# Rows of an RMSNorm + SiLU kernel dealt out to partitions in another order: 64 consecutive rows for each partition

## The chip, the cores and the metric

The kernel runs on one core of one Trainium2 chip. The metric is the device time of one execution in microseconds (us); lower is better. Three runs of the kernel before took 316.70, 317.02 and 317.08 us, so its median is 317.02 us.

The engines that matter here are ScalarE (ACT in the profile), VectorE (DVE), SyncE (SP, which only issues transfers in this kernel) and the core's 16 DMA engines, which move all data between the device memory and the core's on-chip memory. The on-chip memory has 128 partitions. TensorE (PE) is used once, at the start, to copy one row to all partitions.

## The reference

```python
batch, seq_len, hidden = 8, 1024, 2048          # x: (8, 1024, 2048) float32, gamma: (2048,)

def reference(x, gamma, eps):
    rms = np.sqrt(np.mean(x ** 2, axis=-1, keepdims=True) + eps)
    out = gamma * x / rms
    return (out * (1 / (1 + np.exp(-out)))).astype(np.float32)
```

Flattened, x is an array of 8192 rows of 2048 float32 values, 8 KB a row and 67.1 MB in all. Each row is computed by itself: its root mean square, the division by it, the multiplication by gamma, and SiLU. The output has the same shape. So 67.1 MB are read and 67.1 MB are written, and any assignment of rows to partitions computes the same thing as long as the output is written by the same assignment.

## The kernel before, in words

**Tiling.** The 8192 rows are cut into `nblk` = 16 blocks. A block has 128 partitions with `J` = 4 rows each: 512 rows, 4 MB, in one tile `xt` of 128 x 8192 float32. Six such buffers exist (`BUFS` = 6). A load (`load`, line 54) brings one whole block in with one transfer, issued from ScalarE's queue; a store (`store`, line 102) writes one whole block out, issued from SyncE's queue. Results are written in place, so a store reads the buffer that the load filled.

**Where a block lies in memory.** Lines 35 and 36 give the views `xb` and `ob` of x and out. In the kernel before, the rows are numbered block first, then partition, then row in the partition. Partition p of block b holds the rows 512 b + 4 p to 512 b + 4 p + 3. Its four rows are one run of 32 KB, and the 128 runs of a block follow one another, so a block is one piece of 4 MB.

**Work on a block.** Each of a block's four rows per partition is squared and summed, some of them on ScalarE (`squares_scalar`, line 65) and some on VectorE (`squares_vector`, line 73). `root` (line 82) takes the square root of the mean on ScalarE, `invert` (line 87) the reciprocal on VectorE, `multiply` (line 92) multiplies each row by its reciprocal and by gamma on VectorE, and `silu` (line 98) applies SiLU on ScalarE in two halves of a block and then issues the store. The last block takes another form of the same arithmetic (lines 152 to 158), so that its store can be issued early.

**Order.** The order is written out by hand (`manual_schedule`). Load 0 is issued first, then gamma is loaded from SyncE's queue (line 110) and copied to all partitions by TensorE (line 113); load 1 and then loads 2 to 5 follow on ScalarE's queue. In the loop over blocks, the squares of block b + 1 stand beside the multiplication and SiLU of block b. Load b + 3 is issued by ScalarE behind its first squares of block b + 1 (line 69), from b = 3 on, into the buffer that the store of block b - 3 must have left.

Of the kernel before, what the change touches and what calls it, by code (L numbers as in the profile page):

```python
# [1 line left out]

# [4 lines left out]

ACT = mybir.ActivationFunctionType
ALU = mybir.AluOpType


@with_exitstack
def kernel(
    ctx: ExitStack,
    tc: tile.TileContext,
    x: bass.AP,
    gamma: bass.AP,
    eps: bass.AP,
    out: bass.AP,
):  # L20

    nc = tc.nc
    P = nc.NUM_PARTITIONS
    f32 = mybir.dt.float32
    x2 = x.flatten_outer_dims()
    o2 = out.flatten_outer_dims()  # L30
    n, d = x2.shape
    J = 4
    BUFS = 6
    nblk = n // (P * J)
    xb = x2.rearrange("(b p j) d -> b p (j d)", p=P, j=J)
    ob = o2.rearrange("(b p j) d -> b p (j d)", p=P, j=J)

    singles = ctx.enter_context(tc.tile_pool(name="singles", bufs=1))
    pool = ctx.enter_context(tc.tile_pool(name="pool", bufs=BUFS))
    small = ctx.enter_context(tc.tile_pool(name="small", bufs=2))  # L40
    psum = ctx.enter_context(tc.tile_pool(name="psum", bufs=1, space=bass.MemoryType.PSUM))

    Q = 4
    w = d // Q
    g = singles.tile([P, d], f32)
    eps_t = singles.tile([P, 1], f32)
    ones = singles.tile([P, P], f32)
    junk_a = psum.tile([P, d], f32, name="junk_a")
    junk_v = psum.tile([P, d], f32, name="junk_v")
    blocks, sss, rmss, rstds = {}, {}, {}, {}  # L50

    def load(b):
        xt = pool.tile([P, J * d], f32, name="xt")
        nc.scalar.dma_start(out=xt, in_=xb[b])  # L54
        blocks[b] = xt

    def row(b, j):
        return blocks[b][:, j * d:(j + 1) * d]

    def squares_scalar(b, loads=()):  # L60


        sss[b] = small.tile([P, J], f32, name="ss")
        for j in range(share(b)):
            nc.scalar.activation(out=junk_a, in_=row(b, j), func=ACT.Square,  # L65
                                 accum_out=sss[b][:, j:j + 1])
            if j == 0:
                for s in loads:
                    load(s)

    def squares_vector(b):
        for j in range(share(b), J):
            nc.vector.tensor_tensor_reduce(  # L73
                out=junk_v, in0=row(b, j), in1=row(b, j), scale=1.0, scalar=0.0,
                op0=ALU.mult, op1=ALU.add, accum_out=sss[b][:, j:j + 1])

    def share(b):
        return 1 if 4 <= b <= 12 and b % 2 == 0 else 2

    def root(b):  # L80
        rms = small.tile([P, J], f32, name="rms")
        nc.scalar.activation(out=rms, in_=sss.pop(b), func=ACT.Sqrt, scale=1.0 / d, bias=eps_t)  # L82
        rmss[b] = rms

    def invert(b):
        rstd = small.tile([P, J], f32, name="rstd")
        nc.vector.reciprocal(out=rstd, in_=rmss.pop(b))  # L87
        rstds[b] = rstd

    def multiply(b):  # L90
        for j in range(J):
            nc.vector.scalar_tensor_tensor(out=row(b, j), in0=row(b, j), scalar=rstds[b][:, j:j + 1],  # L92
                                           in1=g, op0=ALU.mult, op1=ALU.mult)

    def silu(b):
        for h in range(0, J, 2):
            cols = slice(h * d, (h + 2) * d)
            nc.scalar.activation(out=blocks[b][:, cols], in_=blocks[b][:, cols], func=ACT.Silu)  # L98
        store(b)

    def store(b):
        nc.sync.dma_start(out=ob[b], in_=blocks[b])

    with tc.manual_schedule():

        load(0)
        nc.vector.memset(ones, 1.0)  # L107
        nc.vector.memset(eps_t, float(eps))
        nc.scalar.activation(out=junk_a[:, 0:1], in_=ones[:, 0:1], func=ACT.Square)  # L109
        nc.sync.dma_start(out=g[0:1, :], in_=bass.AP(tensor=gamma.tensor, offset=gamma.offset, ap=[[d, 1], [1, d]]))  # L110
        for c in range(Q):
            cols = slice(c * w, (c + 1) * w)
            nc.tensor.matmul(junk_v[:, cols], ones[0:1, :], g[0:1, cols], start=True, stop=True)  # L113
        load(1)
        nc.vector.tensor_copy(out=g, in_=junk_v)  # L115
        nc.scalar.copy(out=junk_a[:, 0:1], in_=junk_v[:, d - 1:d])  # L116
        for b in range(2, BUFS):
            load(b)

        last = nblk - 1
        SOON = 3
        squares_scalar(0)
        squares_vector(0)
        root(0)
        invert(0)
        for b in range(last):
            loads = [b + 3] if BUFS <= b + 3 < nblk else []
            if b < SOON:  # L130
                multiply(b)
                squares_scalar(b + 1, loads)
                silu(b)
                squares_vector(b + 1)
                root(b + 1)
            elif b < last - 1:
                squares_scalar(b + 1, loads)
                squares_vector(b + 1)
                root(b + 1)
                multiply(b)  # L140
                silu(b)
            else:
                multiply(b)
                squares_scalar(b + 1)
                silu(b)
                squares_vector(b + 1)
                root(b + 1)
            if b + 1 < last:
                invert(b + 1)


        for j in range(J):
            if j == J // 2:
                invert(last)
            nc.vector.tensor_mul(out=row(last, j), in0=row(last, j), in1=g)  # L155
        for j in range(J):
            nc.scalar.activation(out=row(last, j), in_=row(last, j), func=ACT.Silu,  # L157
                                 scale=rstds[last][:, j:j + 1])
        store(last)


# [1 line left out]
_INS = ['x', 'gamma', 'eps']  # L163
_OUTS = [((8, 1024, 2048), 'float32')]

_NUMBERS = {'eps': 9.999999747378752e-06}


# [26 lines left out]
```

## Time and profile before

| | |
|---|---|
| time, median of 3 runs | 317.02 us (316.70 to 317.08) |
| profiled execution: its span, first to last instruction | 315.1 us |
| VectorE busy | 235.3 us (75%) |
| ScalarE busy | 213.9 us (68%) |
| bytes moved | 134.24 MB, mean 426 GB/s over the span |
| one load, issue to landing, median | 38.7 us |
| one store, issue to landing, median | 29.0 us |

The profile's page shows one execution. Its span is counted from the first to the last instruction, so the time that a run reports is a little longer: here 317.02 us at the median against a span of 315.1 us. The page gives no separate total time for the profiled execution.

How to read the lines that follow. The page's "busy" line has, for each engine, busy us, share of the span and number of instructions. The rows under the heading of 40 slices cut the span into 40 equal pieces of 7.88 us; a digit is the busy share in tenths, and the GB/s row has the bytes that landed in each slice. A line of the queues has the number of packets, the megabytes, and the time that the packets took as a share of 16 engines over the span; q10 carries the loads of x, q1 the stores and gamma. The chain is the series of waits and instructions that ended last, followed back from the end, as shares of the span. A line of the waits reads: engine, what was about to run and its line, what it waited for, us in total, how often, the longest.

### The profile page before, as it was taken

The page shows a single profiled execution, that of the slowest core. Times are in us where ns is not written, and L with a number is a line of the kernel's source. Part 1 is how long each engine was busy: PE and PEld are TensorE (multiplying, and loading weights), DVE is VectorE, ACT ScalarE, POOL GpSimd, SP SyncE. Part 2 cuts the span into 40 slices and gives each one's busy share as a digit, 9 for nine tenths or more (in the row PEclk, how much of TensorE's full clock was granted, in tenths as well). Part 3 has the DMA queues.
Part 4 walks back from the last instruction along what each step waited for, and adds up shares of the span by engine and source line. Part 5 has one row for each costly group of instructions (what it writes and reads, how often), then busy time and mean ns, then how long its engine had stood idle before and what let it go on. Part 6 is the DMA issues. An engine that isn't in the chain of part 4 may idle for free.

```text
span 315.1 us, 439 instructions
## 1 busy us (share of the span) xinstructions
PE 7.2 (2%) x8; PEld 2.5 (1%) x8; DVE 235.3 (75%) x157; ACT 213.9 (68%) x137; POOL 0.2 (0%) x4
## 2 busy tenths in 40 slices
PE   6200000000000000000000000000000000000000
PEld 2000000000000000000000000000000000000000
DVE  0679697979895695957969489593995939999600
ACT  1269998972799258682687827877278768779910
POOL 0000000000000000000000000000000000000000
DMA  8999999999999999999999999999999999999997
GB/s 334 412 453 416 383 458 408 462 403 462 403 459 408 454 412 458 408 462 403 462 403 462 408 458 408 458 408 458 416 449 416 449 416 449 428 437 428 437 428 308
DMA packets 4613, 134.24 MB, mean 426 GB/s; under 512 B 514, under 2 KB 514, under 8 KB 514
## 3 DMA queue, kind: packets, MB, share of 16 engines
q10 hardware_dynamic: 2304, 67.11, 49.8%
q1 hardware_dynamic: 2306, 67.12, 49.3%
q14 instruction: 3, 0.02, 0.0%
HBM read 67.12 MB, written 67.11 MB: 426 GB/s over the span
## 4 chain that ended last, share of the span: by engine, by line
DMA 68%; DVE 14%; ACT 11%; issue 1%; ACTq 1%; DVEq 0%
DMA xt<-in_x_dram 68%; DVE xt L92 9%; DVE junk_v L73 5%; ACT xt L98 4%; ACT junk_a L65 3%; ACT xt L157 2%; ACT L82 1%; ACTq L190 1%; ACT L157 0%; ACT L98 0%; ACT rms L82 0%; DVE ss L73 0%; ACTq L54 0%; DVE rstd L87 0%; ACT L109 0%
## 5 line engine op out<-in xcount | busy, mean ns | idle before, releaser
L92 DVE SCALAR_TENSOR_TENSOR xt<-xt,rstd,g 128x2048 f32<-128x2048 f32 x60 | 137.0, 2346 | 0.1
L98 ACT ACTIVATE xt<-xt 128x4096 f32<-128x4096 f32 x30 | 108.3, 3615 | 27.4 <-DVE xt L92 27.4
L73 DVE CUSTOM_DVE_ANT_0 junk_v<-xt 128x2048 f32<-128x2048 f32 x37 | 85.1, 2299 | 42.9 <-DMA xt<-in_x_dram 42.2
L65 ACT ACTIVATE junk_a<-xt 128x2048 f32<-128x2048 f32 x27 | 50.7, 1876 | 16.1 <-DMA xt<-in_x_dram 14.0
L82 ACT ACT_TABLE_LOAD x15 | 19.2, 1283 | 26.6 <-DVE ss L73 26.5
L98 ACT ACT_TABLE_LOAD x14 | 18.0, 1283 | 0.2
L115 DVE COPY g<-junk_v 128x2048 f32<-128x2048 f32 x1 | 2.3, 2292 | 9.0 <-PE junk_v L113 9.0
L87 DVE RECIPROCAL rstd<-rms 128x4 f32<-128x4 f32 x16 | 2.7, 172 | 8.4 <-ACT rms L82 8.4
L155 DVE TENSOR_TENSOR xt<-xt,g 128x2048 f32<-128x2048 f32 x4 | 8.9, 2277 | 0.0
L82 ACT ACTIVATE rms<-ss,eps_t 128x4 f32<-128x4 f32 x16 | 4.8, 297 | 5.7 <-DVE ss L73 5.5
L157 ACT ACTIVATE xt<-xt,rstd 128x2048 f32<-128x2048 f32 x4 | 7.7, 1991 | 0.0
L113 PE MATMUL junk_v<-g,ones 1*128 1x512 f32 x8 | 7.2, 1072 | 2.8 <-DMA g<-in_gamma_dram 2.8
L116 ACT COPY junk_a<-junk_v 128x1 f32<-128x1 f32 x1 | 0.1, 144 | 9.8 <-DVE g L115 9.8
L73 DVE DVE_READ_ACCUMULATOR2_ANT ss<- 128x1 f32 x37 | 5.2, 141 | 0.0
L65 ACT ACTIVATION_READ_ACCUMULATOR junk_a<-xt 128x1 f32 x27 | 5.0, 186 | 0.0
L113 PEld LDWEIGHTS junk_v<-g,ones 1*128 1x128 f32 x8 | 2.5, 325 | 5.9 <-issue 5.9
L109 ACT ACT_TABLE_LOAD x1 | 1.3, 1283 | 1.1 <-PEq L176 1.1
L157 ACT ACT_TABLE_LOAD x1 | 1.3, 1283 | 0.0
L107 DVE MEMSET ones<- 128x128 f32 x1 | 0.2, 165 | 0.8 <-PEq L176 0.8
L109 ACT ACTIVATE junk_a<-ones 128x1 f32<-128x1 f32 x1 | 0.2, 174 | 0.0
L176 POOL MEMSET const-bfloat16-1.0<- 128x1 bf16 x1 | 0.1, 103 | 0.0
L176 POOL MEMSET const-uint8-127<- 128x1 uint8 x1 | 0.1, 102 | 0.0
(3 smaller groups left out, 0.3 us busy)
## 6 DMA issues: line engine op xcount, KB each, us to landing
xt<-in_x_dram ACTq DMA_DIRECT2D x16, 4096.0 KB, 38.7
out_dram<-xt SPq DMA_DIRECT2D x16, 4096.0 KB, 29.0
g<-in_gamma_dram SPq DMA_DIRECT2D x1, 8.0 KB
```

Source lines behind the costliest of these rows:

```text
L65: nc.scalar.activation(out=junk_a, in_=row(b, j), func=ACT.Square, accum_out=sss[b][:, j:j + 1])
L73: nc.vector.tensor_tensor_reduce(out=junk_v, in0=row(b, j), in1=row(b, j), scale=1.0, scalar=0.0, op0=ALU.mult, op1=ALU.add, accum_out=sss ...
L82: nc.scalar.activation(out=rms, in_=sss.pop(b), func=ACT.Sqrt, scale=1.0 / d, bias=eps_t)
L87: nc.vector.reciprocal(out=rstd, in_=rmss.pop(b))
L92: nc.vector.scalar_tensor_tensor(out=row(b, j), in0=row(b, j), scalar=rstds[b][:, j:j + 1], in1=g, op0=ALU.mult, op1=ALU.mult)
L98: nc.scalar.activation(out=blocks[b][:, cols], in_=blocks[b][:, cols], func=ACT.Silu)
L109: nc.scalar.activation(out=junk_a[:, 0:1], in_=ones[:, 0:1], func=ACT.Square)
L113: nc.tensor.matmul(junk_v[:, cols], ones[0:1, :], g[0:1, cols], start=True, stop=True)
L115: nc.vector.tensor_copy(out=g, in_=junk_v)
L155: nc.vector.tensor_mul(out=row(last, j), in0=row(last, j), in1=g)
L157: nc.scalar.activation(out=row(last, j), in_=row(last, j), func=ACT.Silu, scale=rstds[last][:, j:j + 1])
L190: with _tile.TileContext(nc) as tc:
```

## The change

The two views are rearranged with the partition first, then the block, then the row in the partition.

```diff
     nblk = n // (P * J)
-    xb = x2.rearrange("(b p j) d -> b p (j d)", p=P, j=J)
-    ob = o2.rearrange("(b p j) d -> b p (j d)", p=P, j=J)
+    xb = x2.rearrange("(p b j) d -> b p (j d)", p=P, j=J)
+    ob = o2.rearrange("(p b j) d -> b p (j d)", p=P, j=J)
```

Now partition p holds the rows 64 p to 64 p + 63 over the whole kernel, and block b takes the rows 64 p + 4 b to 64 p + 4 b + 3 of every partition. A partition's share of a block is still one run of 32 KB. The starts of neighbouring partitions' runs are 64 rows apart, 512 KB, and no longer 32 KB. The runs of one block are spread over the whole array, and the next block's runs lie directly behind them. Loads and stores use the same assignment. Nothing else in the kernel is touched: the transfers are as many, of the same sizes, on the same queues and in the same order.

## The prediction

> **What bounds the kernel now.** I read the page of the profiled execution first (shares, transfers, chain), then the waits, then a table of the span cut into stretches.
>
> The page's opening, the transfer rows under the 40 slices, its queues and its chain:
>
> ```profile
> span 315.1 us, 439 instructions
> PE 7.2 (2%) x8; PEld 2.5 (1%) x8; DVE 235.3 (75%) x157; ACT 213.9 (68%) x137; POOL 0.2 (0%) x4
> ...
> DMA  8999999999999999999999999999999999999997
> GB/s 334 412 453 416 383 458 408 462 403 462 403 459 408 454 412 458 408 462 403 462 403 462 408 458 408 458 408 458 416 449 416 449 416 449 428 437 428 437 428 308
> DMA packets 4613, 134.24 MB, mean 426 GB/s; under 512 B 514, under 2 KB 514, under 8 KB 514
> ...
> q10 hardware_dynamic: 2304, 67.11, 49.8%
> q1 hardware_dynamic: 2306, 67.12, 49.3%
> ...
> DMA 68%; DVE 14%; ACT 11%; issue 1%; ACTq 1%; DVEq 0%
> ```
>
> The 16 DMA engines are busy in every slice but the first and the last, while VectorE (DVE) is busy for 75% and ScalarE (ACT) for 68% of the span. The chain that ended last is 68% loads. So the transfers set the pace. The waits say the same from the other side: the longest waits of the two computing engines on anything outside themselves are for loads.
>
> ```profile
> DVE junk_v L73 <- DMA xt<-in_x_dram: 42.2, 11, 5.7
> ...
> ACT junk_a L65 <- DMA xt<-in_x_dram: 14.0, 7, 2.7
> ```
>
> VectorE waits 42.2 us in 11 places for a block to land before its square sums on line 73, ScalarE 14.0 us in 7 places on line 65. Those waits are slack: if transfers slow down, the two engines wait longer and take nothing from anybody.
>
> Next, what one packet costs. The load queue q10 carries 2304 packets: 16 transfers of 128 data runs of 32 KB, and 16 small packets more for each transfer. Its share is 49.8% of 16 engines over 315.1 us, so 0.498 x 16 x 315.1 / 2048 = 1.226 us for a run that is loaded; for the store queue q1, 0.493 x 16 x 315.1 / 2048 = 1.214 us. Each engine handles 4096 / 16 = 256 runs, one after the other, and 256 x 1.21 = 310 us is nearly the span. Whatever changes the time of one 32 KB run changes the kernel's time 256 times over.
>
> The span cut into stretches (columns: from and to; width; busy us of PE, PEld, DVE, ACT, POOL; clock; DMA share; GB/s):
>
> ```profile
> 4.00:36.00 32.00, 5.94 (x7) 1.75 (x6) 20.95 (x14) 18.97 (x15) 0.00 (x0) 1.00 0.99 429
> 36.00:42.00 6.00, 0.00 (x0) 0.00 (x0) 5.17 (x4) 5.93 (x7) 0.00 (x0) 1.00 0.95 350
> 42.00:280.00 238.00, 0.00 (x0) 0.00 (x0) 192.53 (x128) 166.74 (x102) 0.00 (x0) 1.00 1.01 434
> 280.00:300.90 20.90, 0.00 (x0) 0.00 (x0) 16.46 (x11) 20.79 (x13) 0.00 (x0) 1.00 0.99 428
> ```
>
> From 4 to 36 us there are loads only (the first store is issued at 35.2 us): 429 GB/s. From 42 to 280 us loads and stores share the engines half and half: 434 GB/s. A read-only and a mixed stretch run at one rate, so in this layout the memory's mix of work does not set the 1.21 us; something the engines have in common does. The exception is the 6 us in which the first store joins: 350 GB/s at a DMA share of 0.95. That is 350 x 6 = 2.10 MB in place of 434 x 6 = 2.60 MB, a loss of 0.50 MB, or 1.16 us at 434 GB/s. The engines were hardly idle there, so the runs themselves took longer: 0.95 x 16 x 6 us over 2.10 MB / 32 KB = 64 runs gives 1.42 us for one. It is the one place where the trace shows a run slowed by something outside its engine.
>
> **The change, part by part.** Nothing is added or removed in the instruction streams: 16 load issues on ScalarE's queue and 16 stores on SyncE's, 128 runs of 32 KB each, in the same order and behind the same waits; VectorE, ScalarE and TensorE do the same work on the same tile shapes. These cost 0, without any cover being needed. The permutation of rows over partitions is the same for load and store. The row gamma is loaded as before. A partition's run stays whole at 4 rows = 32 KB, so I expect 2304 packets again.
>
> What changes is where the runs lie in memory. Before, the 128 runs of a transfer follow each other and fill one stretch of 4 MB. After, each starts 512 KB after the last, so a transfer touches the whole 64 MB array, and the 16 engines, which step through their runs together, always work at places that are equal modulo 512 KB up to their progress within a run. The proof that they step together is in the slices: the rate alternates between about 403 and 462 GB/s, which over 7.88 us is 3.18 and 3.64 MB, near 6 and 7 rounds of 16 runs of 32 KB (0.524 MB each). If the memory spreads its work by the address bits that the runs now have in common, the 16 engines crowd onto few of its parts.
>
> No row of this trace has runs at that pitch, so the price is bounded from both sides.
> - **Lower end.** The steady rate cannot rise by the change if the read-only stretch and the mixed one already agree to 1% with sequential runs. What can go is the dip at 36 to 42 us: -1.16 us. So the gain is at most about 1.2 us.
> - **Upper end.** Every run is as slow as those of the dip. 134.24 MB take 134.24 / 0.434 = 309.3 us at the steady rate and 134.24 / 0.350 = 383.5 us at the dip's: +74.2 us.
> - **The value taken.** The steady row holds 238 us, the dip 6 us, so the value must lie near the lower end. I put one run in eight at the dip's price, as if of the eight runs that an engine has in each transfer the first, at which it moves to a new part of the array, were the one that collides: 74.2 / 8 = 9.3 us. This eighth is a choice, not a reading; the ends are kept for the range.
>
> The Trainium skill speaks against the change. "DMA: Bandwidth & Descriptors", section "Latency and other measured facts", lists copies with 128 partitions of 16 KiB at a row pitch that is a large power of two: 207 GB/s in each direction at 512 KiB, 164 at 2 MiB, 103 at 4 MiB, against 214 with a padded pitch. No row of this trace has such a pitch. Taken as 207 against 214, the 309.3 us would become an estimated 319.8 us, +10.5 us, and the kernel 327.5 us. The page calls its explanation, engines in lock step that meet on the same channels of the memory, an inference.
>
> **The sum.** The profiled execution's span is 315.1 us; the median of the runs is 317.02 us, so 1.9 us lie around the span. 315.1 + 9.3 = 324.4 us of span, and 324.4 + 1.9 = 326.3 us. Call it 326 us. What the span holds beside the 309.3 us (its start, the dip, the last receipt: 5.8 us) is taken as unchanged.
>
> **The rivals.**
> - **The memory has room: no change.** For it: 429 and 434 GB/s in stretches with unlike work, and runs that hold 1.21 us for 240 us together. Against it: those rows have sequential runs only, and the dip shows that the memory side can stretch a run. It gives 317.0 us, within 0.2% (0.6 us, about what a measurement of this kernel can tell from no change).
> - **The dip goes: faster.** Place: 36 to 42 us, where the first store joins the loads. Price: 1.16 us. Before, load and store streams lie in separate 4 MB pieces; spread over the arrays they may meet more evenly. It gives 317.02 - 1.16 = 315.9 us. It decides only as long as the steady rate holds: at 434 x 309.3 / (309.3 + 1.16) = 432.4 GB/s the gain is used up. Against it: the dip may be the store queue's start and no matter of addresses.
> - **The crowding is general: much slower.** If half of the runs pay the dip's price, 74.2 / 2 = 37.1 us, 354 us; all of them, 391 us. For it: the pitch is the same in every transfer, load and store, so nothing within a transfer cures it. Against it: a 32 KB run passes over many small addresses within 1.21 us, and engines that are held up fall out of step and then collide less.
> - **The change does not do what it says.** If the runs were cut differently, for instance at a row of 8 KB, the packets would be four times as many; there are already 514 small packets in 315 us without a visible price. The contiguous inner 32 KB speaks against it.
>
> **How the numbers follow.** Chances: the forecast, with its own range from one run in sixty to one run in four at the dip's price (+1.2 to +18.6 us, 318 to 336 us), 0.50; no change 0.16; the dip goes 0.12; general crowding, above 336 us, 0.20; other cuts, slower, 0.02. So faster 0.12, same 0.16, slower 0.72. The range of 315.5 to 354 us, from the faster rival to half of the runs at the dip's price, holds nearly all of the first three cases and half of the fourth, some 0.87 in all; to cut it shorter would leave out either the faster rival or the crowding, whose price nothing in the trace pins down.
>
> **What would show it right or wrong.** Right: 2304 packets on q10 again, the DMA row of the slices still full, but the stretch from 42 to 280 us near 421 GB/s (434 x 309.3 / 318.6) and each queue's time per run near 1.25 us; the waits of line 73 for loads longer, VectorE's and ScalarE's busy time as before. The no-change rival shows 434 GB/s and 1.21 us; the faster one shows 434 with the 36 to 42 us stretch filled; general crowding shows a rate under 400 GB/s. The prediction is wrong if the rate holds in every stretch, or if a queue's shares diverge, loads slowed and stores not, so that the price falls on one direction alone: then half of the sum, some 4.6 us, would be left.

## The result and the profile after

The changed kernel takes 322.03 us (median of 6 runs, 319.94 to 323.86) against 317.03 us for the kernel before (6 runs, 316.70 to 317.15). The ratio is 1.016, with a 95% interval of 1.0146 to 1.0174: 5.0 us slower. The runs also lie further apart than before, 3.9 us from lowest to highest against 0.45 us.

The profiled execution of the changed kernel is the slowest of the six: 323.86 us, with a span of 322.1 us. So its trace shows 7.0 us more span than that of before, 2.0 us more than the median lost; what is split up below are these 7.0 us. The page's opening, the rows under the 40 slices, the queues and the chain:

```profile
span 322.1 us, 439 instructions
PE 7.2 (2%) x8; PEld 2.5 (1%) x8; DVE 235.4 (73%) x157; ACT 214.1 (66%) x137; POOL 0.2 (0%) x4
...
DMA  8999999999999999999999999999999999996994
GB/s 318 427 427 435 387 419 435 440 415 440 431 420 444 423 420 444 423 435 431 431 431 427 431 435 419 435 431 435 431 423 423 431 444 411 427 435 301 444 403 203
...
q10 hardware_dynamic: 2304, 67.11, 49.3%
q1 hardware_dynamic: 2306, 67.12, 48.3%
...
DMA xt<-in_x_dram 69%; DVE xt L92 8%; ACT xt L98 5%; DVE junk_v L73 5%; ACT junk_a L65 3%; ACT xt L157 2%; ACT L82 1%; ACTq L190 1%; ACT L157 0%; ACT L98 0%; ACT rms L82 0%; DVE ss L73 0%; DVE rstd L87 0%; ACTq L54 0%; ACT L109 0%
```

Three things are to be seen. The packets are the same in number, 2304 and 2306, so the transfers were cut as before. The engines' busy time is the same (VectorE 235.4, ScalarE 214.1 us). And the GB/s row has lost its pattern: before, it alternated between about 403 and 462, a sign of 16 engines that finish their 32 KB runs together; now it wanders around 430, a sign of engines out of step. (Late in the kernel before the pattern fades too, to 428 and 437, so it is no proof; the landings below are better evidence.) Near the end stands a hole (a DMA digit of 6, 301 GB/s) that the kernel before does not have.

The shares turn into time per run as in the prediction: a loaded run takes 0.493 x 16 x 322.1 / 2048 = 1.241 us (1.226 before), a stored run 0.483 x 16 x 322.1 / 2048 = 1.215 us (1.214 before). Only loads got slower, by 0.015 us on average. Over the 128 loaded runs of an engine that is 1.9 us, not 7.

The same stretches as before (columns: from and to; width; busy us of PE, PEld, DVE, ACT, POOL; clock; DMA share; GB/s), changed kernel:

```profile
4.00:36.00 32.00, 6.08 (x8) 1.90 (x6) 20.96 (x14) 18.56 (x15) 0.00 (x0) 1.00 1.00 433
36.00:42.00 6.00, 0.00 (x0) 0.00 (x0) 4.76 (x4) 5.94 (x7) 0.00 (x0) 1.00 0.98 350
42.00:280.00 238.00, 0.00 (x0) 0.00 (x0) 187.16 (x127) 163.37 (x102) 0.00 (x0) 1.00 1.00 430
280.00:300.90 20.90, 0.00 (x0) 0.00 (x0) 19.84 (x12) 17.85 (x11) 0.00 (x0) 1.00 0.91 390
```

As long as only loads run, the new layout costs nothing: 433 GB/s from 4 to 36 us, where the kernel before had 429. The dip at 36 to 42 us is there again, at 350. The steady stretch has 430 in place of 434, the stretch from 280 us on 390 in place of 428.

Where the 7.0 us come from shows in the chain of waits in order of time. Each piece is the time (start, us) in which the chain ran through loads alone; the three last pieces of before, then of after:

```profile
143.81 38.65 DMA xt<-in_x_dram
182.50 38.67 DMA xt<-in_x_dram
...
240.56 38.64 DMA xt<-in_x_dram
```

```profile
146.45 39.16 DMA xt<-in_x_dram
205.48 40.28 DMA xt<-in_x_dram
245.79 40.35 DMA xt<-in_x_dram
```

In such a piece two blocks are loaded and two stored; it has grown from 38.65 to as much as 40.35 us. The last starts 5.2 us later than before and ends at 286.14 us (245.79 + 40.35) against 279.20 us (240.56 + 38.64): 6.9 us later. What follows, the arithmetic of the last block and its store, takes 322.1 - 286.1 = 36.0 us and took 315.1 - 279.2 = 35.9 us. So the whole loss is the later landing of the last load.

Each load ends in the trace with 16 small packets of 4 bytes, which are read here as one for each engine, sent when its part is done. For the last load of the kernel before, all 16 stand in a window from 276.5 to 278.9 us:

```profile
DMA packets 48, 1.05 MB, mean 437 GB/s; under 512 B 16, under 2 KB 16, under 8 KB 16
...
q10 hardware_dynamic: 16, 0.00, 0.4%
```

They start from 278.01 to 278.85 us there, and from 277.08 to 285.77 us after the change. The first is even earlier than before; the last is 6.9 us later, and it is the last that the waiting engines go by (the chain has the landing at 286.14 us). Before, the spread between the first and the last is never over 0.8 us. After, it is 0.8 us at the first load, 4.4 at the eighth, 5.5 at the twelfth, 8.7 us at the last: some parts fall further and further behind. The queues of the changed kernel in the 6.7 us after 279.2 us, when before all loads were done and no packet of q10 was left:

```profile
DMA packets 105, 2.95 MB, mean 440 GB/s; under 512 B 15, under 2 KB 15, under 8 KB 15
...
q10 hardware_dynamic: 13, 0.20, 6.8%
```

0.20 MB are 6 runs that late engines still have to load, and everything waits for them. At the other end, engines that were not late run out of work. Changed kernel, two short stretches near the end:

```profile
294.00:298.00 4.00, 0.00 (x0) 0.00 (x0) 3.83 (x2) 3.98 (x2) 0.00 (x0) 1.00 0.38 164
...
318.70:320.80 2.10, 0.00 (x0) 0.00 (x0) 0.00 (x0) 0.00 (x0) 0.00 (x0) 1.00 0.04 16
```

From 294 to 298 us the engines are 38% busy, since the earlier stores are out and the last blocks' arithmetic is late. From 318.7 us on a share of 0.04 is less than one engine of 16: the rest wait for the last one. Put together by the shares, the 16 engines were busy with the two queues for 97.6% of 322.1 = 314.4 us after and 99.1% of 315.1 = 312.3 us before. Of the 7.0 us, 2.1 are longer runs and 4.9 are engines that have nothing to do.

### The profile page after: what moved, and what is told of

The parts are those of the page before. It is cut to its first block, busy times and chain, and to the rows that moved or that the text cites. A ratio compares the mean times of both kernels' runs of the same rounds, so it can differ in the third digit from the quotient of the medians.

```text
span 322.1 us, 439 instructions
## 1 busy us (share of the span) xinstructions
PE 7.2 (2%) x8; PEld 2.5 (1%) x8; DVE 235.4 (73%) x157; ACT 214.1 (66%) x137; POOL 0.2 (0%) x4
## 3 DMA queue, kind: packets, MB, share of 16 engines
q10 hardware_dynamic: 2304, 67.11, 49.3%
q1 hardware_dynamic: 2306, 67.12, 48.3%
## 4 chain that ended last, share of the span: by engine, by line
DMA 69%; DVE 14%; ACT 12%; ACTq 1%; issue 1%; DVEq 0%
DMA xt<-in_x_dram 69%; DVE xt L92 8%; ACT xt L98 5%; DVE junk_v L73 5%; ACT junk_a L65 3%; ACT xt L157 2%; ACT L82 1%; ACTq L190 1%; ACT L157 0%; ACT L98 0%; ACT rms L82 0%; DVE ss L73 0%; DVE rstd L87 0%; ACTq L54 0%; ACT L109 0%
```

## The experiments

**One side at a time.** Which transfers must have the new layout for the price to appear? First the stores alone, then the loads alone.

```diff
-    ob = o2.rearrange("(b p j) d -> b p (j d)", p=P, j=J)
+    ob = o2.rearrange("(p b j) d -> b p (j d)", p=P, j=J)
```

> Loads as before (one piece of 4 MB), stores as in the change (runs 512 KB apart); each result row is thus written at the place of another row. In the changed kernel only the load runs took longer (1.24 us against 1.226 by the queue's share), and only from the moment the first store had joined. Theory C (it is the scattered stores that hold up loads): 322 us, last load landing near 286 us, loads' time per run near 1.24 us. Theory D (it is the loads' own pitch): 317 us, last load near 279 us. Theory A (a power-of-two pitch on both sides, so that a load and a store meet at places equal modulo 512 KB): between, 317 to 319 us.

Measured: 319.43 us, ratio 1.007 (1.0049 to 1.0091).

```diff
-    xb = x2.rearrange("(b p j) d -> b p (j d)", p=P, j=J)
+    xb = x2.rearrange("(p b j) d -> b p (j d)", p=P, j=J)
```

> Loads as in the change (runs 512 KB apart), stores as before (one piece of 4 MB); each result row is thus written at the place of another row. Theory C (scattered stores hold up loads): 317 us. Theory D (the loads' own pitch): 322 us. Theory A (both sides must have the pitch): 317 to 319 us. All three expect the stretch from 4 to 36 us, where only loads run, at 429 to 434 GB/s as in both kernels so far.

Measured: 319.17 us, ratio 1.0068 (1.0053 to 1.0083). By the ratios each side alone costs 2.2 us (0.7% of 316.88 us; by the medians 2.5 and 2.3 us), and the two together make 4.4 us, near the 5.0 us of the whole change. Theories C and D fall. Theory A's time is just missed from above, and its ground, that both sides must have the pitch, is wrong: one is enough. The profile of the first is of its fastest run (317.50 us; the five others took 318.89 to 319.82), so it is not read here. The queues of the second, loads far apart:

```profile
q10 hardware_dynamic: 2304, 67.11, 49.7%
q1 hardware_dynamic: 2306, 67.12, 49.0%
```

With its span of 317.4 us a loaded run takes 0.497 x 16 x 317.4 / 2048 = 1.232 us, a stored one 1.215 us. Again the loads are the ones that are held up. The two queues keep the engines busy for 98.7% of the span, 313.3 us: of the 2.3 us more span, 1.0 are longer runs, and here too the larger part is engines without work.

**A pitch that is no power of two.** The array is spread almost as widely, but a partition has 60 consecutive rows in place of 64, and the rows that remain make one sequential block.

```diff
+    def cut(a):
+        far = a[0:7680].rearrange("(p b j) d -> b p (j d)", p=P, j=J)
+        near = a[7680:8192].rearrange("(p j) d -> p (j d)", j=J)
+        return [far[b] for b in range(15)] + [near]
+    xb = cut(x2)
+    ob = cut(o2)
```

> Runs of one transfer lie 480 KB apart (15 blocks), and the last block is one piece of 4 MB. The array is spread almost as widely as in the change, but the pitch is no power of two. Theory A (power of two): back to 317 us, last load landing near 279 us, the 16 parts of each landing within about 1 us. Theory B (any layout in which a transfer's runs are not neighbours costs the same): 322 us, or a little under it for the one block that is whole, and the landing spread out to some 8 us at the end.

Measured: 316.85 us, ratio 0.9999 (0.999 to 1.0009). Its rate row, between slices of about 399 and 466 almost to the end:

```profile
span 315.0 us, 439 instructions
...
GB/s 334 404 462 404 395 466 399 466 399 466 399 467 399 463 404 462 404 462 404 462 404 462 408 458 408 458 408 458 412 454 412 454 416 449 420 445 424 441 429 308
```

The engines stay in step, and the last load's parts land within 0.8 us, from 277.9 to 278.7 us. (In this and the later expectations theory A is that of the power of two.) That settles it between A and B: runs that are scattered over the whole array cost nothing, runs that are scattered at 512 KB do.

**Other pitches.** 256 KB, from two halves of the array with 8 blocks each:

```diff
+    def cut(a):
+        halves = [a[h * 4096:(h + 1) * 4096].rearrange("(p b j) d -> b p (j d)", p=P, j=J)
+                  for h in range(2)]
+        return [halves[b // 8][b % 8] for b in range(16)]
+    xb = cut(x2)
+    ob = cut(o2)
```

> The array is cut into two halves of 8 blocks; the runs of one transfer lie 256 KB apart. Theory A (power of two, the worse the larger the pitch): 318 to 321 us. Theory B (any spread costs the same): 322 us. If 256 KB costs nothing, 317 us, then the price begins between 256 and 512 KB.

Measured: 317.30 us, ratio 1.0011 (1.0001 to 1.0021), so 0.4 us, less than theory A had thought. 384 KB, for 12 blocks, with 4 sequential blocks behind them:

```diff
+    def cut(a):
+        far = a[0:6144].rearrange("(p b j) d -> b p (j d)", p=P, j=J)
+        near = a[6144:8192].rearrange("(b p j) d -> b p (j d)", p=P, j=J)
+        return [far[b] for b in range(12)] + [near[b] for b in range(4)]
+    xb = cut(x2)
+    ob = cut(o2)
```

> Runs of a transfer 384 KB apart for 12 blocks; the last 4 blocks are one piece of 4 MB each. So far 256 KB cost about 0.4 us, 512 KB 5 us and 480 KB nothing. Theory A1 (what counts is at how many different places modulo 512 KB the runs of one transfer lie: one at a pitch of 512 KB, two at 256 KB, four here, sixteen at 480 KB): under 0.4 us, so 316.8 to 317.2 us. Theory A2 (the price grows with the pitch as such and 480 KB was a lucky size): 12/16 of something between 0.4 and 5 us, 318 to 320 us.

Measured: 316.95 us, ratio 1.0001 (0.9992 to 1.001). So it is not the distance: 384 and 480 KB, which 12 and 15 of the 16 blocks had, are free, 256 KB costs 0.4 us, 512 KB 5.0 us. The four prices follow the number of different places modulo 512 KB at which a transfer's runs begin: four and sixteen of them, free; two, 0.4 us; one, 5.0 us. The largest power of two that divides the pitch orders them the same way; these runs do not tell the two readings apart.

**Reads among reads.** Is it the pitch alone, or must reads and writes meet? The first 15 stores become second loads of the same block into the same buffer; first with the change, then, as a control, in the kernel before.

```diff
-        nc.sync.dma_start(out=ob[b], in_=blocks[b])
+        if b < nblk - 1:
+            nc.sync.dma_start(out=blocks[b], in_=xb[b])
+        else:
+            nc.sync.dma_start(out=ob[b], in_=blocks[b])
```

> The change, with the first 15 stores replaced by a second load of the same block into the same buffer, so that all transfers but the last are reads and 15 of 16 blocks of the result are not written. The waits and the bytes moved stay. In the changed kernel the first 36 us, loads only, ran at 433 GB/s. Theory M (a run is held up only where reads and writes meet): 317 us, landings within about 1 us. Theory R (streams of runs at this pitch hold each other up, also reads among reads): 319 to 323 us, landings spread out to several us.

> The same replacement of 15 stores by second loads in the kernel before: the control for the run with the change. Both theories: 316 to 317 us. If it is itself slower than 317.5 us, the replacement costs something of its own, and the run with the change has to be read against this one.

Measured: 317.47 us, ratio 1.0016 (1.0007 to 1.0025), with the change; 317.41 us, ratio 1.0015 (1.0006 to 1.0024), without. The replacement costs 0.5 us by itself, and the pitch adds 0.06 us, nothing that can be told from zero. The last load's parts spread over 2.3 us with the change and 1.5 us without, a little more than theory M said, but nowhere near 8.7. Theory R falls: engines that step through reads at 512 KB pitch together do not hold each other up. The stretches with the change:

```profile
4.00:36.00 32.00, 5.56 (x7) 1.66 (x5) 20.95 (x14) 18.48 (x15) 0.00 (x0) 1.00 1.01 434
36.00:42.00 6.00, 0.00 (x0) 0.00 (x0) 4.67 (x3) 5.94 (x7) 0.00 (x0) 1.00 0.99 426
42.00:280.00 238.00, 0.00 (x0) 0.00 (x0) 192.81 (x129) 166.81 (x103) 0.00 (x0) 1.00 1.00 432
```

The dip at 36 to 42 us is gone too: 426 GB/s, and 437 in the control, where every kernel that stores whole blocks has 339 to 382. So the dip is the first writes meeting reads, and not the start of a second queue.

**Moving the stores against the loads.** If it mattered at which places of the 512 KB the loads and the stores are at together, moving one against the other would change the price.

```diff
-        nc.sync.dma_start(out=ob[b], in_=blocks[b])
+        nc.sync.dma_start(out=ob[(b + 8) % nblk], in_=blocks[b])
```

> The change, with each block stored at the place of the block 8 further on (modulo 16), so that loads and stores that run together are 256 KB further apart modulo 512 KB; result rows are written at the places of other rows. Theory P (what counts is which places of the 512 KB the loads and the stores are at together): a clear move, under 319.5 or over 325 us. Theory Q (the pitch of each side counts by itself, as the two half changes with +2.5 us each suggest): 322 us as the change.

> The changed kernel once more, beside the three others. Expected by every theory: 320 to 324 us, last load landing near 286 us, and the 16 parts of that landing spread out over several us, as in the first profile (8.7 us between the first and the last of the 16 engines). If the spread is small and the time still 322 us, the account that one late engine sets every landing is wrong.

Measured: 320.38 us, ratio 1.0137 (1.0091 to 1.0183), for the moved stores; 321.61 us, ratio 1.0143 (1.0092 to 1.0193), for the change once more. The two cannot be told apart, which speaks for theory Q; with four runs each, a difference of some 2 us would not show. The second profile of the change repeats the first: a span of 321.7 us, the last load's parts from 277.9 to 285.4 us, a spread of 7.5 us. Like the first it is of the slowest run (323.45 us), so no trace shows the change at its median. The profile of the moved stores is of their fastest run (319.62 us): a span of 317.8 us, a spread of 3.9 us. Together with the loads alone (317.4 us, 2.8 us), the kernel before (315.1 us, 0.8 us) and the first profile of the change (322.1 us, 8.7 us), the span goes with the spread.

**A larger pitch.** To make the suspected cause stronger, each block was cut into four transfers of 32 partitions with their runs 2 MB apart, and for control into four sequential pieces.

```diff
-    xb = x2.rearrange("(b p j) d -> b p (j d)", p=P, j=J)
+    xb = x2.rearrange("(p i b j) d -> b i p (j d)", i=4, p=32, j=J)   # control: (b i p j) d
...
-        nc.scalar.dma_start(out=xt, in_=xb[b])
+        for i in range(4):
+            nc.scalar.dma_start(out=xt[32 * i:32 * i + 32, :], in_=xb[b, i])
```

(the view `ob` and the store in the same way)

> Each block's transfer is cut into four of 32 partitions, and the runs of one such transfer lie 2 MB apart; loads and stores alike, the result is in its place. Theory A (the price comes with the power of two of the pitch and grows with it): well over the change, 330 us or more. If the price depends on the number of different places that a transfer visits modulo 512 KB and not on the pitch: 322 us plus what the cutting costs, which the run with sequential quarters shows.

> The kernel before, with each block's transfer cut into four of 32 partitions, each one sequential piece of 1 MB: the control for quarters at 2 MB pitch. 96 more issues of 0.33 us, half of them on ScalarE's queue, which is 68% busy: 317 to 319 us.

Measured: 460.44 us, ratio 1.4524 (1.45 to 1.4547), at 2 MB; 468.64 us, ratio 1.4674 (1.4575 to 1.4774), for the sequential control. The control's expectation failed by far: the cutting itself costs some 150 us. At 2 MB the time is over the 330 us of theory A, but not for its reason, since the control without the pitch is no faster. The control's stretch with loads alone:

```profile
4.00:36.00 32.00, 6.09 (x8) 1.89 (x6) 7.01 (x5) 0.39 (x3) 0.00 (x0) 1.00 1.01 208
```

208 GB/s at full DMA engines, half of the 429 before. With the transfers limited elsewhere, this says nothing on the price of a pitch of 2 MB, which stays open.

## Why the prediction was right, and where it was not

**The bound.** Right: transfers set the pace, the computing engines' busy time did not change, and their waits for loads grew, as the two lines of the waits after the change show.

```profile
DVE junk_v L73 <- DMA xt<-in_x_dram: 47.8, 11, 6.1
...
ACT junk_a L65 <- DMA xt<-in_x_dram: 17.8, 8, 3.0
```

**What the change does.** Right: 2304 packets again, and a price that comes from where the runs lie. The pitch of 480 KB shows that it is the common place modulo a power of two, which the prediction gave as its condition ("if the memory spreads its work by the address bits that the runs now have in common"). Half of its picture is wrong: the 16 engines do not crowd each other as long as they only read (433 GB/s from 4 to 36 us, and 317.47 against 317.41 us with reads alone). Nor do writes alone pay much: behind the last load a stored run took 1.218 us on average, against 1.213 before. Reads and writes must meet.

**The bounds.** The lower end, a gain of 1.2 us if the dip went, did not happen: the dip stands at 350 GB/s in both. That the row for the upper end was of the right kind is luck: the prediction took the dip as a run slowed from outside its engine, and the run without stores showed later that it, too, needs writes beside reads. The packets of the dip show it as well: before, its load runs took 1.505 us on average and its store runs 1.213 us.

**The size.** The term of the sum that was mis-sized is "one run in eight at the dip's price", 9.3 us; 5.0 us were measured, some 7% of the 74.2 us to the upper end. The eighth was a choice, and the traces do not bear out its picture, in which an engine's first run in each transfer collides. After 42 us, no load run of the kernel before took over 1.23 us. In the changed kernel 89 of 1552 took over 1.3 us, 1.49 on average, and of these only 1 was among the first 16 runs of its load. Most come where a store begins: 59 of the 89 started within 4 us of a store's first run, where an even spread would have 18 (stores begin some 19.4 us apart), and in the second profile 63 of 90. So something like the dip, which the kernel before has at its first store alone, comes back at later stores. It is not the whole condition: of the fewer long runs with the loads alone, the stores alone and the moved stores, 1 of 14, 4 of 30 and 14 of 50 stood there. The rate predicted for the steady stretch, 421 GB/s, was 430. The sum also had the wrong form: it added up an average stretch of all runs, and that average, 2.1 us in the profile, is the smaller part. The rest, 4.9 us, is unevenness: the delays gather on some engines, and a transfer lands with its last engine. The prediction had falling out of step only as a relief ("engines that are held up fall out of step and then collide less"); here it is the larger part of the price. That 326 us came near 322 is thus partly luck, and the stated range, 315.5 to 354 us, left much room.

**The last sentence.** The case in which "the price falls on one direction alone" was put down as one that would prove the prediction wrong, at "some 4.6 us". It is the one that came: loads at 1.241 us, stores at 1.215. By its own sign, then, the prediction had this part of the mechanism wrong, though its time fell in the range. Its 4.6 us are near the 5.0 measured, but not for its reason, since half the runs at the dip's price is no mechanism that was found.

**The rivals.** No change would have been right at 384 or 480 KB, and nearly at 256 KB. General crowding never came near: the steady stretch lost 1%, where that rival had its rate under 400 GB/s.

**The rule.** The Trainium skill, "DMA: Bandwidth & Descriptors", section "Latency and other measured facts", had the right sign. The estimate worked out from its figures, +10.5 us, is twice what was measured here, where the runs are 32 KB and not 16 KB. It says that a large power-of-two pitch padded by 4 KiB runs at the full rate again; the pitch of 480 KB, which is off the power of two by 32 KB, agrees (316.85 us). It calls the meeting of lock-stepped streams an inference; here streams of reads alone at that pitch had no price (317.47 us against 317.41).

What stays open is where in the memory the reads and the writes meet, why the loads pay and the stores do not, and why some engines collect more delay than others: the trace does not name the engine of a packet.

## What to carry to other kernels

In these runs a transfer had landed only with its last engine. In a kernel bound by transfers, compare when the 16 parts of a late load land, not only the mean rate: here 1% of rate in the steady stretch and 0.015 us a run became 5 us, because the delays gathered on some engines. Where a layout puts the runs of one transfer 512 KB apart and reads and writes run together, move the pitch off it, for instance to 60 rows in place of 64; the distance itself was free. What larger powers of two cost was not measured here.

## What had not been expected of the hardware

Reads at a pitch of 512 KB ran at full rate beside other reads and lost rate only beside writes, and no difference was seen between the sides that had the pitch: 2.2 us for each. The other finding is the price of transfers over 32 partitions: 16 full DMA engines moved 208 GB/s, against 429 GB/s with 128 partitions, in pieces of 1 MB with the same runs of 32 KB. The Trainium skill, "SBUF — State Buffer", section "Door 1: The DMA port swizzle", says that the rate depends on how many of the on-chip memory's 16 ports the partitions reach, and by its table 32 neighbouring partitions reach 8; the measured half agrees.
